# Two operands of the RWKV-7 chunk products on halves of the partitions, q ahead of the triangular inverse, and sums of squares loaded by 32 columns

## The chip, the cores and the metric

The kernel runs on one core of a Trainium2 chip. The metric is the device time of one execution in microseconds (us). The core has TensorE (PE; its weight loads are listed as PEld), VectorE (DVE), ScalarE (ACT), GpSimd (POOL) and SyncE (SP, which issues most DMAs). A tile of TensorE's array is named by rows and columns: 64*64 is one quarter, given by the half of the partitions that the operands lie on and the half that the result goes to in PSUM.

## The reference, cut to what matters

Two layers: dilated window attention, then RWKV-7 time mixing, each with attention into memory tokens, a gate and an output projection. There are 512 prompt tokens and 8 x 4 sample tokens. The change lies in the RWKV layer (12 heads of 64) and in the sums of squares of the norms.

```python
kk = k * k_k
kk = kk / jnp.maximum(jnp.sqrt(jnp.sum(kk * kk, axis=-1, keepdims=True)), 1e-12)
k = k * (1.0 + (a - 1.0) * k_a)
def step(S, inp):            # inp: r, decay, k, v, -kk, kk * a
    r_t, w_t, k_t, v_t, a_t, b_t = inp
    sa = einsum('bhvk,bhk->bhv', S, a_t)
    S = S * w_t[:, :, None, :] + sa[..., None] * b_t[:, :, None, :] + v_t[..., None] * k_t[:, :, None, :]
    return S, einsum('bhvk,bhk->bhv', S, r_t)
y = x * lax.rsqrt(jnp.mean(x * x, axis=-1, keepdims=True) + 1e-6) * g      # every norm
```

## The kernel before

All activations are held feature-major: features on partitions, the 544 tokens along the free axis. Dense products (lines 314 to 316) split weights and activations into a high and a low float32r part and add three products into one PSUM bank.

The scan of the 512 prompt tokens is done in 8 chunks `c` of 64. Two heads `h` fill one tile of 128 features; two such pairs `j` make a group `g`, so there are three groups of four heads. Per pair, `decay` and `keys` (L1289) form A, R (tile AR) and B, K (tile BK). `keys` first needs the sum of squares of each head: five matmuls named kn (L1304) load 128 tokens of the squares (the last 32) and stream the two columns of `ind2`. Norms do the same over all features in `add_squares` (L325; tiles ss, ssm, ssz).

`scores` (L1349) makes, for each chunk and head, the 64x128 products of B and of K with A and R. Masked, they stand in SA (with A) and SR (with R), index 0 from B and 1 from K; `unit` and `score` say on which half of the partitions and in which columns the block of a chunk and head lies. Then `by_token` transposes A and v into UV and B and K into BK, 128x128 at a time.

`products` (L1429) inverts the triangular 64x64 blocks of a group. A loop of 30 steps on DVE (L1477, L1479) inverts 32x32 blocks, X (L1493, L1502) joins them, and SA holds the inverse. Behind it stand, of 32 matmuls each: w, the inverse with A (L1513); q, the scores of K with v (L1528); v, the inverse with q (L1528). Each takes two PSUM banks of the tag "t", which has two buffers, and two copies. `recur` (L1640) then goes through the chunks: z takes the state `St` to the next chunk, y gives the output; DVE adds what z gave into `u` (L1703) and makes the new state (L1721).

Work is recorded by generators with ranks (class `Flow`): the one with the lowest rank that is ready goes next, and dense products fill between. The program's order is then set by a scheduler that plays the recorded program through a timeline of its own, so an edit in one place can move instructions elsewhere. `by_turns` keeps the matmuls of one token in the order written. On the chip each engine runs its own list strictly in order.

The last group's recurrence ends the RWKV layer. Dense products of the output projection stand beside it: o1 (12 records for each of 16 results; they need the gated features 0 to 3 of groups 0 and 1) and o2 (which needs group 2), then the last norm (ssz) and the stores.

Of the kernel before, what the change touches and what calls it, by code (L numbers as in the profile page):

```python
# [54 lines left out]
NT = 544  # L55
# [177 lines left out]
def _device(tc, I, O):  # L233
# [91 lines left out]
    def add_squares(acc, sq, n, first, last):  # L325

        for i in (0, 256, 128) if n > 256 else (0, 128):
            w = min(128, n - i)
            nc.tensor.matmul(acc[0:w, i // 128:i // 128 + 1], sq[:, i:i + w], ones[:, 0:1],
                             start=first and i == 0, stop=last and i == 128)  # L330
# [899 lines left out]
    def unit(c, j, h):  # L1230
        a = ((c - j) % 8 // 2 * 2 + h) * 64
        return H2[(c + j) % 2], slice(a, a + 64)


    def turned(c, j, h):
        return h ^ (c + j) % 2

    def score(c, j, h):
        a = ((c - j) % 8 // 2 * 2 + turned(c, j, h)) * 64
        return H2[(c + j) % 2], slice(a, a + 64)  # L1240

    def block(i, j, e):

        return (2 * i + j, e), ((2 * i + j + 1) % 8, 1 - e)
# [48 lines left out]
    def keys(p):  # L1293
# [8 lines left out]
        for t in range(5):  # L1302
            w = 128 if t < 4 else 32
            nc.tensor.matmul(pss[0:w, 2 * t:2 * t + 2], sq[:, t * 128:t * 128 + w], ind2, start=True, stop=True)  # L1304
# [45 lines left out]
    def scores(p):  # L1350
# [19 lines left out]
        def by_token(src0, src1, dst, dsts, name):  # L1370

            for x, (src, a) in enumerate((src0, src1)):
# [19 lines left out]

        for i in (0, 2):
            pts = [ps_t(f"sc{n}{i}{e}") for e in range(2)]
            for k in range(2):
                for x in range(2):
                    a = (2 * k + x) * 128
                    for e in (1, 0):
                        for c, h in block(i + k, j, e)[::1 - 2 * e]:
                            nc.tensor.matmul(pts[e][unit(c, j, h)[0], a:a + 128], BK[H2[h], j, x, CH[c]],  # L1400
                                             AR[H2[h], j, :, CH[c]], start=True, stop=True)
                            by_turns(f"sc{n}{i}")
# [22 lines left out]
        yield from by_token((AR.rearrange("p j x t -> p (j x t)"), 2 * j * NT), (q.xv, 0), lambda x: UV[:, x, j], st.UVs[:, j], "av")  # L1425
        flow.done(f"tokens{p}", 1.0)
        flat = BK.rearrange("p j x t -> p (j x t)")
# [3 lines left out]
    Q0, Q1 = [slice(64 * hh, 64 * hh + 32) for hh in range(2)], [slice(64 * hh + 32, 64 * hh + 64) for hh in range(2)]  # L1431

    def products(g):
# [72 lines left out]
        yield f"tokens{2 * g + 1}"  # L1506
        for e in range(2):
            pt = ps_t(f"w{g}{e}")
            for j in range(2):
                for i in range(4):  # L1510
                    for c, h in block(i, j, e):
                        a = (4 * j + i) * 64
                        nc.tensor.matmul(pt[H2[h], a:a + 64], UV[unit(c, j, h)[0], 0, j, unit(c, j, h)[1]],  # L1513
                                         SA[unit(c, j, h)[0], 0, j, score(c, j, h)[1]], start=True, stop=True)
            both[e](AR[:, :, 0, 0:512].rearrange("p j (i e t) -> p j i e t", e=2, t=64)[:, :, :, e],
                    pt.rearrange("p (j i t) -> p j i t", j=2, t=64))
            yield 1.0, 0

        u = st.u = UV[:, 0].rearrange("p j (c e v) -> p (j c) e v", c=4, e=2)
        for k in range(2):  # L1520
            for i in range(2):
                pt = ps_t(f"{'qv'[k]}{g}{i}")
                for c in range(4 * i, 4 * i + 4):
                    for j, h in PAIRS:
                        r, cs = score(c, j, h)
                        e = turned(c, j, h)
                        a = (c % 4 * 2 + e) * 64
                        nc.tensor.matmul(pt[r, a:a + 64], SA[r, 1 - k, j, cs],  # L1528
                                         u[r, c, e] if k else UV[r, 1, j, unit(c, j, h)[1]], start=True, stop=True)
                both[i](UV[:, 0, i], pt)  # L1530
                yield 1.0, 0
# [116 lines left out]
    def recur(g):  # L1648
# [19 lines left out]
        def y_of(cs, e):  # L1668
# [7 lines left out]
            for step in steps:  # L1676
                c, k, t = step
                for j, h in PAIRS:
                    if turned(c, j, h) == t:
                        r, s = score(c, j, h)  # L1680
                        lhs = SR[r, 2 - k, j, s] if k else AR[H2[h], j, 1, CH[c]]
                        rhs = (UV[r, 1, j, unit(c, j, h)[1]] if k == 1 else u[r, c, t] if k else states[c][H2[h], j ^ h])
                        y = ((c - a) * 2 + h) * 64
                        put(yps[r, y:y + 64], lhs, rhs, e and step == steps[0], not e and step == steps[-1])
# [11 lines left out]
        for c in range(8):  # L1696
            n = f"{g}_{c}"
            states.append(St)
            if c:
                for j, h in PAIRS:  # L1700
                    r, cs = score(c, j, h)
                    put(zs[r, turned(c, j, h), 0, c % 2], AR[H2[h], j, 0, cs], St[H2[h], j ^ h], True, True)
# [10 lines left out]
            for k in (1, 0):  # L1713
                for j, h in PAIRS:
                    r, cs = unit(c, j, h)
                    e = turned(c, j, h)
# [330 lines left out]
```

## Time and profile before

| | us |
|---|---|
| median of 3 runs | 797.19 |
| all runs | 796.6, 803.0, 797.19 |
| the profiled execution | 796.88 |
| its span on the core | 794.9 |
| mean granted TensorE clock | 0.976 |

A row of the profile names line, engine, operation, result and operands, then how many, and durations. In a timeline row stand the start, the time to the end of the last record, and the idle time ahead of it with what ended that. An f32 matmul of TensorE stands as two records, a transpose or a float32r matmul as one. The granted clock is the share of full clock that TensorE was given. The chain of waits is followed back from the last instruction.

### The profile page before, as it was taken

How to read it: one execution, taken by the hardware profiler on the slowest of the kernel's cores; microseconds unless marked ns; L12 is line 12 of the kernel's file. 1: busy time of each engine (PE TensorE's matmuls, PEld its weight loads, DVE VectorE, ACT ScalarE, POOL GpSimd, SP SyncE). 2: the span in 40 equal slices, each digit the busy share in tenths (PEclk: the TensorE clock that was granted, in tenths of full speed). 3: DMA queues.
4: the chain of work that ended last, by engine and by line, in shares of the span. 5: the costliest groups of instructions: out<-in, count | busy, mean ns of one | idle time of the engine just before them, and what ended most of it. 6: DMA issues, size and time to landing. Idle time of an engine off the chain costs nothing.

```text
span 794.9 us, 20301 instructions
## 1 busy us (share of the span) xinstructions
PE 740.0 (93%) x8360; PEld 631.8 (79%) x8360; DVE 444.2 (56%) x1088; ACT 338.3 (43%) x789; POOL 349.4 (44%) x389
## 2 busy tenths in 40 slices
PE   6899999999999969889999999899999999999783
PEld 5877878798976857788888889798888987888663
DVE  7743321218455574652545479837599455785456
ACT  7454421125443464447585348243644423621121
POOL 4642322332220554755444337534455345551447
PEclk9999999999999999999999999999999999999797
DMA  7465359862225571254114421210223222540103
GB/s 251 132 221 180 114 176 310 305 242 84 82 68 218 185 242 42 76 162 134 55 47 149 151 89 61 77 41 16 71 74 108 84 82 82 154 130 19 51 31 114
DMA packets 55697, 97.49 MB, mean 123 GB/s; under 512 B 6607, under 2 KB 21231, under 8 KB 55567
## 3 DMA queue, kind: packets, MB, share of 16 engines
q1 hardware_dynamic: 55604, 96.19, 37.1%
q8 instruction: 66, 1.08, 0.6%
q14 instruction: 27, 0.22, 0.1%
HBM read 82.67 MB, written 13.49 MB: 121 GB/s over the span
## 4 chain that ended last, share of the span: by engine, by line
PE 72%; DVE 12%; POOL 5%; DMA 4%; issue 3%; ACT 3%; SPq 1%; POOLq 0%; DVEq 0%; ACTq 0%
PE b_h L314 2%; PE b_h L315 2%; PE b_h L316 2%; PE o L314 2%; PE Sx L566 2%; PE o L315 2%; PE o L316 2%; PE sc L1400 2%; PE y L1663 1%; PE z L1663 1%; PE o L794 1%; PE ox L590 1%; DMA ug<-ud 1%; PE ptx L582 1%; DMA vc<-in_vc 1%
## 5 line engine op out<-in xcount | busy, mean ns | idle before, releaser
L307 POOL TENSOR_TENSOR lo_b<-raw_b,hi_b 128x512 fp32r<-128x512 f32 x58 | 77.6, 1340 | 119.8 <-ACT hi_b L306 88.2
L307 POOL TENSOR_TENSOR lo_a<-raw_a,hi_a 128x512 fp32r<-128x512 f32 x44 | 56.7, 1290 | 130.2 <-ACT hi_a L306 129.6
L306 ACT CAST hi_a<-raw_a 128x512 fp32r<-128x512 f32 x44 | 27.3, 621 | 61.7 <-DMA raw_a<-in_w_in_a 34.6
L306 ACT CAST hi_b<-raw_b 128x512 fp32r<-128x512 f32 x58 | 36.4, 628 | 38.1 <-PE b_h L316 10.0
L315 PE MATMUL b_h<-xg,lo_b 128*128 128x272 f32 x160 | 46.1, 296 | 2.0 <-POOL lo_b L307 2.0
L314 PE MATMUL b_h<-xg,hi_b 128*128 128x272 f32 x160 | 47.3, 301 | 0.0
L316 PE MATMUL b_h<-xg,hi_b 128*128 128x272 f32 x160 | 46.1, 294 | 0.0
L314 PEld LDWEIGHTS b_h<-xg,hi_b 128*128 128x128 f32 x160 | 29.8, 188 | 3.8 <-issue 2.3
L315 PEld LDWEIGHTS b_h<-xg,lo_b 128*128 128x128 f32 x160 | 29.8, 188 | 3.0 <-POOL lo_b L307 2.4
L1477 DVE TENSOR_TENSOR TX<-T,TT 128x30 f32<-128x30 f32 (+14 forms) x90 | 29.3, 326 | 3.9 <-ACT T L1451 2.2
L1479 DVE TENSOR_TENSOR T<-T,TX 128x30 f32<-128x30 f32 (+14 forms) x90 | 30.0, 333 | 1.8
L316 PEld LDWEIGHTS b_h<-xg,hi_b 128*128 128x128 f32 x160 | 29.8, 188 | 0.5
L1705 POOL TENSOR_TENSOR Sd<-St,DF 128x128 f32<-128x128 f32 x21 | 8.4, 402 | 36.5 <-DVE St L1723 19.0
L1400 PE MATMUL sc<-AR,BK 64*64 64x128 f32 x384 | 18.2, 277 | 1.9 <-DVE bv L1346 1.9
L314 PE MATMUL o<-h,hi_o1a 128*128 128x256 f32 (+1 forms) x64 | 18.7, 293 | 0.9 <-DVE z L1941 0.9
L316 PE MATMUL o<-h,hi_o1a 128*128 128x256 f32 (+1 forms) x64 | 18.4, 290 | 0.9 <-DVE h L1797 0.9
L315 PE MATMUL o<-h,lo_o1a 128*128 128x256 f32 (+1 forms) x64 | 18.4, 288 | 0.0
L786 ACT COPY PT<-pa 128x512 f32<-128x512 f32 x16 | 9.1, 586 | 21.8 <-PE pa L785 17.9
L1663 PE MATMUL y<-UV,SR 64*64 64x64 f32 x384 | 17.3, 242 | 0.0
L1400 PEld LDWEIGHTS sc<-AR,BK 64*64 64x64 f32 x384 | 12.4, 133 | 5.0 <-DVE bv L1346 2.3
L1663 PEld LDWEIGHTS y<-UV,SR 64*64 64x64 f32 x384 | 15.7, 157 | 0.3 <-issue 0.3
L1721 DVE TENSOR_TENSOR St<-z,Sd 128x128 f32<-128x128 f32 x21 | 6.0, 286 | 16.2 <-PE z L1663 11.6
(1066 smaller groups left out, 2796.2 us busy)
## 6 DMA issues: line engine op xcount, KB each, us to landing
raw_b<-in_w_in_b SPq DMA_DIRECT2D x58, 256.0 KB, 2.7
raw_a<-in_w_in_a SPq DMA_DIRECT2D x44, 256.0 KB, 2.8
kc<-in_kc SPq DMA_DIRECT2D x18, 512.0 KB, 6.4
vc<-in_vc SPq DMA_DIRECT2D x18, 512.0 KB, 7.6
out_win<-t SPq DMA_DIRECT2D x12, 272.0 KB, 3.0
x<-in_x SPq DMA_DIRECT2D x8, 272.0 KB, 5.4
xr<-in_x SPq DMA_DIRECT2D x16, 136.0 KB, 4.2
x1d<-z SPq DMA_DIRECT2D x2, 1088.0 KB, 5.2
```

The lines of the kernel that those rows point to most:

```text
L306: nc.scalar.copy(hi, raw)
L307: lo_eng.tensor_tensor(lo, raw, hi.bitcast(F32), ALU.subtract)
L314: nc.tensor.matmul(ps[:, :n], hi, xh, start=first, stop=False)
L315: nc.tensor.matmul(ps[:, :n], lo, xh, start=False, stop=False)
L316: nc.tensor.matmul(ps[:, :n], hi, xl, start=False, stop=last)
L566: nc.tensor.matmul(S[hh][64 * e:64 * e + 64, 0:256], qm[r, f, a:a + 64], kT[l][r, f, :], start=True, stop=True)
L786: nc.scalar.copy(PT[hh], pa.rearrange("p (j q) -> p j q", j=4))
L1400: nc.tensor.matmul(pts[e][unit(c, j, h)[0], a:a + 128], BK[H2[h], j, x, CH[c]], AR[H2[h], j, :, CH[c]], start=True, stop=True)
L1477: nc.vector.tensor_tensor(pd, TP[:, 0:s, s:s + 1].to_broadcast([128, s, w]), TT[:, s:s + 1, s + 1:32].to_broadcast([128, s, w]), ALU.mult)
L1479: nc.vector.tensor_tensor(TP[:, 0:s, s + 1:32], TP[:, 0:s, s + 1:32], pd, ALU.add)
L1663: nc.tensor.matmul(out, lhs, rhs, start=start, stop=stop)
L1705: nc.gpsimd.tensor_tensor(Sd, St, DF[:, :, c:c + 1].to_broadcast([128, 2, 64]), ALU.mult)
```

## The change

Five edits:

1. `add_squares` and kn load 32 columns at a time and write to partitions 0, 32, 64 and 96 in turn: kn has 17 matmuls in place of 5, the squares of the last norm 27 and 24 in place of 9 and 6.
2. The scores with A of head 1 go to the other half of the partitions than those with R. For that the 64x128 product with B is cut in two of 64x64; ten matmuls take the place of eight.
3. A and v are transposed by half tiles (64 rows, 128 tokens) in `two_by_two`, so that A of head 1 lands on the other half. 17 or 19 matmuls take the place of 8 or 10.
4. q moves out of `products` into `early_q`, begun when A and v of the group's second pair have been transposed. Its result `u` goes into the place of the scores in SA, which so lives until the recurrence ends; before, `u` was in UV.
5. In `products` v comes ahead of w, both in the order of `PAIRS` with all four quarters in turn; v uses the two banks "zs" and w two of "t".

The recurrence has the same matmuls with other indices.

```diff
     def add_squares(acc, sq, n, first, last):
         for i in (0, 256, 128) if n > 256 else (0, 128):
-            w = min(128, n - i)
-            nc.tensor.matmul(acc[0:w, i // 128:i // 128 + 1], sq[:, i:i + w], ones[:, 0:1],
-                             start=first and i == 0, stop=last and i == 128)
+            for a in range(0, min(128, n - i), 32):
+                w = min(32, n - i - a)
+                nc.tensor.matmul(acc[a:a + w, i // 128:i // 128 + 1], sq[:, i + a:i + a + w], ones[:, 0:1],
+                                 start=first and i == 0, stop=last and i == 128)
...
+    def low(c, j, h=0):
+        return (c + j + h) % 2
+    def slot(c, e):
+        a = (c // 2 * 2 + e) * 64
+        return slice(a, a + 64)
+    def tokens(c, j, h, odd):
+        a = ((c - odd) % 8 // 2 * 2 + h) * 64
+        return slice(a, a + 64)
     PAIRS = ((0, 0), (1, 1), (1, 0), (0, 1))
...
-            nc.tensor.matmul(pss[0:w, 2 * t:2 * t + 2], sq[:, t * 128:t * 128 + w], ind2, start=True, stop=True)
+            for a in range(0, 128 if t < 4 else 32, 32):
+                nc.tensor.matmul(pss[a:a + 32, 2 * t:2 * t + 2], sq[:, t * 128 + a:t * 128 + a + 32], ind2, start=True, stop=True)
...
+        def two_by_two():
...
+            for x, (src, a) in enumerate(((src0, a0), (src1, a1))):
+                for i in range(4):
+                    for h, r in enumerate(H2):
+                        odd = low(0, j, 0 if x else h)
+                        o_, b = pts[h][:, (4 * x + i) * 64:(4 * x + i) * 64 + 64], a + 128 * i + 64 * odd
...
+                        nc.tensor.transpose(o_, src[r, b:b + o_.shape[0]], ident[r, r])
...
             for k in range(2):
-                for x in range(2):
-                    a = (2 * k + x) * 128
-                    for e in (1, 0):
-                        for c, h in block(i + k, j, e)[::1 - 2 * e]:
-                            nc.tensor.matmul(pts[e][unit(c, j, h)[0], a:a + 128], BK[H2[h], j, x, CH[c]],
-                                             AR[H2[h], j, :, CH[c]], start=True, stop=True)
+                cs, a = (2 * (i + k), 2 * (i + k) + 1), 256 * k
+                for c in cs:
+                    piece(0, c, 0, None, low(c, j), a)
+                    piece(1, c, 0, 0, low(c, j, 1), a)
+                for c in cs:
+                    piece(1, c, 0, 1, low(c, j), a)
+                for c in cs:
+                    for h in range(2):
+                        piece(h, c, 1, None, low(c, j), a + 128)
...
         flow.done(f"tokens{p}", 1.0)
+        if j:
+            flow.spawn(RANK[3], early_q(g))
...
+    def early_q(g):
+        st.u = SA[:, 1].rearrange("p j (c e v) -> p (j c) e v", c=4, e=2)
+        pts = [ps_t(f"q{g}{b}") for b in range(2)]
+        for c in range(8):
+            for j, h in PAIRS:
+                b = low(c, j)
+                nc.tensor.matmul(pts[b][H2[low(c, j, h)], 64 * c:64 * c + 64], SA[H2[b], 1, j, slot(c, h)],
+                                 UV[H2[b], 1, j, tokens(c, j, h, j)], start=True, stop=True)
+        for b in range(2):
+            both[b](st.u[:, :, b], pts[b].rearrange("p (c v) -> p c v", v=64))
...
-        yield f"tokens{2 * g + 1}"
+        yield f"q{g}"
+        pt = ps_zs(f"v{g}").rearrange("p (e c v) -> p e c v", e=2, v=64)
+        for c in range(8):
+            for j, h in PAIRS:
+                e = low(c, j, h)
+                nc.tensor.matmul(pt[H2[low(c, j)], e, c], SA[H2[e], 0, j, slot(c, h)], u[H2[e], c, low(c, j)],
+                                 start=True, stop=True)
         for e in range(2):
-            pt = ps_t(f"w{g}{e}")
...
+            both[e](u[:, :, e], pt[:, e])
+        pts = [ps_t(f"w{g}{e}") for e in range(2)]
...
```

Three places of TensorE's list show what moves. The first is the first product X of the last group's inverse (X from TX and SA) among the dense o1 products (o from h and hi_o1a or lo_o1a). Before:

```order
L315 MATMUL o_10011<-h_9766,lo_o1a_10008 128x256
L316 MATMUL o_10011<-h_9766,hi_o1a_10007 128x256
L1493 MATMUL X_8923<-TX_8474,SA_7479 32x32 x32
L314 MATMUL o_10025<-h_9766,hi_o1a_10007 128x288
L315 MATMUL o_10025<-h_9766,lo_o1a_10008 128x288
```

And now:

```order
L315 MATMUL o_10100<-h_9985,lo_o1a_10083 128x288
L316 MATMUL o_10100<-h_9985,hi_o1a_10082 128x288
L1546 MATMUL X_9069<-TX_8624,SA_7616 32x32 x32
L314 MATMUL o_10124<-h_9985,hi_o1a_10120 128x256
L315 MATMUL o_10124<-h_9985,lo_o1a_10121 128x256
```

Before, X stood behind the thirteenth of the 16 results of o1, with 132 dense records left behind it in the program; now it stands behind the sixth, with 216 left. Recurrence 1's last z had 407 left and now has 450.

The second place is the end of the same inverse (X from SA and TX) and the products behind it. Before:

```order
L1502 MATMUL X_8973<-SA_7479,TX_8474 32x32 x32
L316 MATMUL o_10063<-h_9766,hi_o1a_10045 128x288
L1513 MATMUL w_9020<-SA_7479,UV_7481 64x64
L1513 MATMUL w_9038<-SA_7479,UV_7481 64x64
L1513 MATMUL w_9020<-SA_7479,UV_7481 64x64 x15
L1513 MATMUL w_9038<-SA_7479,UV_7481 64x64 x15
L1541 MATMUL q2s<-UVs_7483,SAs_7484 32x64 x4
L1528 MATMUL q_9056<-UV_7481,SA_7479 64x64 x16
L1528 MATMUL q_9074<-UV_7481,SA_7479 64x64 x16
L1539 MATMUL w2s<-SAs_7484,UVs_7483 64x32
L1528 MATMUL v_9101<-UV_7481,SA_7479 64x64 x16
L1528 MATMUL v_9119<-UV_7481,SA_7479 64x64 x16
```

And now, behind 24 dense records that follow X:

```order
L316 MATMUL o_10196<-h_9985,hi_o1a_10192 128x256
L1565 MATMUL v_9189<-SA_7616 64x64 x2
L1575 MATMUL w_9224<-SA_7616,UV_7618 64x64 x2
L1565 MATMUL v_9189<-SA_7616 64x64 x30
L1575 MATMUL w_9225<-SA_7616,UV_7618 64x64 x4
L1575 MATMUL w_9224<-SA_7616,UV_7618 64x64 x4
```

q is gone from here, v stands ahead of nearly all of w, and the recurrence's first z follows w; five more results of o1 (60 records) come between its steps.

The third place is the sum of squares kn of the fifth pair among dense products. Before:

```order
L316 MATMUL b5h_7659<-xg_3427,hi_b_7654 128x272
L1304 MATMUL kn_7239<-ind_4288,BK_7003 128x2 x4
L1304 MATMUL kn_7239<-ind_4288,BK_7003 32x2
L314 MATMUL b17h_8122<-xg_3427,hi_b_8112 128x272
L315 MATMUL b17h_8122<-xg_3427,lo_b_8113 128x272
```

And now:

```order
L315 MATMUL b_h_8526<-xg_3475,lo_b_0_8516 128x272
L316 MATMUL b_h_8526<-xg_3475,hi_b_0_8515 128x272
L314 MATMUL b_h_8526<-xg_3475,hi_b_1_8521 128x272
L1302 MATMUL kn_7364<-ind_4336,BK_7023 32x2 x17
L1627 MATMUL gn0s<-ident,yc0s 64x64 x2
```

The 17 small matmuls stand together. SP's list has the load of x1 into SA's buffer behind the store of the last state, where it stood ahead of it, and only stores stand behind it; DVE's list has 31 other instructions inside the last inverse's loop, where it had 36.

More of the change, by code (lines that the diff above doesn't have):

```diff
@@ L1391, in by_token @@
             yield 0.3, 0
+        def two_by_two():
+            (src0, a0), (src1, a1) = (AR.rearrange("p j x t -> p (j x t)"), 2 * j * NT), (q.xv, 0)
+            pts = [ps_t(f"av{n}{h}") for h in range(2)]
+            for x, (src, a) in enumerate(((src0, a0), (src1, a1))):
[3 more added lines that the diff above has]
+                        o_, b = pts[h][:, (4 * x + i) * 64:(4 * x + i) * 64 + 64], a + 128 * i + 64 * odd
+                        if odd and i == 3:
+                            if a:
+                                nc.tensor.transpose(o_, src[r, a - 64:a + 64], ident[r, r])
+                            else:
+                                nc.tensor.matmul(o_[64:128], src[r, 0:64], ident[r, r], start=True, stop=True)
+                            by_turns(f"av{n}")
+                            o_ = o_[0:64]
+                        nc.tensor.transpose(o_, src[r, b:b + o_.shape[0]], ident[r, r])
+                        by_turns(f"av{n}")
+                if not x:
+                    yield 0.5, 0
+            for h in range(2):
+                nc.scalar.copy(UV[:, :, j].rearrange("p x (i e t) -> p x i e t", e=2, t=64)[:, :, :, h],
+                               pts[h].rearrange("p (x i t) -> p x i t", x=2, t=64))
+            yield 0.5, 0
+            yield from by_token((src0, a0), (src1, a1), None, st.UVs[:, j], "av")
@@ L1393, in scores, with piece @@
+        def piece(h, c, x, k, half, a):
+            o_ = a + 64 * (k or 0)
+            rhs = AR[H2[h], j, :, CH[c]] if k is None else AR[H2[h], j, k, CH[c]]
+            nc.tensor.matmul(pts[h][H2[half], o_:o_ + (128 if k is None else 64)], BK[H2[h], j, x, CH[c]], rhs,
+                             start=True, stop=True)
+            by_turns(f"sc{n}")
         for i in (0, 2):
-            pts = [ps_t(f"sc{n}{i}{e}") for e in range(2)]
+            pts = [ps_t(f"sc{n}{i}{h}") for h in range(2)]
@@ L1519, in products @@
[L1519 to L1531, printed above, removed]
+        yield f"q{g}"
@@ new lines, in products @@
+        for c in range(8):
+            for j, h in PAIRS:
+                e, a = low(c, j, h), (4 * j + c // 2) * 64
+                nc.tensor.matmul(pts[e][H2[h], a:a + 64], UV[H2[e], 0, j, tokens(c, j, h, low(0, j, h))],
+                                 SA[H2[e], 0, j, slot(c, h)], start=True, stop=True)
+                by_turns(f"w{g}")
+        for e in range(2):
+            both[1 - e](AR[:, :, 0, 0:512].rearrange("p j (i e t) -> p j i e t", e=2, t=64)[:, :, :, e],
+                        pts[e].rearrange("p (j i t) -> p j i t", j=2, t=64))
```

52 lines of the change are left out of this document (21 added, 31 removed).

## The prediction

> **What bounds the kernel now.** I read the page first: busy shares, slices, and the shares of the chain that ended last.
>
> ```profile
> span 794.9 us, 20301 instructions
> ...
> PE 740.0 (93%) x8360; PEld 631.8 (79%) x8360; DVE 444.2 (56%) x1088; ACT 338.3 (43%) x789; POOL 349.4 (44%) x389
> ...
> PE   6899999999999969889999999899999999999783
> ...
> PEclk9999999999999999999999999999999999999797
> ...
> PE 72%; DVE 12%; POOL 5%; DMA 4%; issue 3%; ACT 3%; SPq 1%; POOLq 0%; DVEq 0%; ACTq 0%
> ```
>
> TensorE holds 72% of the chain, so an instruction saved there counts almost anywhere before the last slices. Then the table by stretches, cut at the marks of the last RWKV group (its inverse starts at 676.4, its first product stands at 718.0, its recurrence runs from 734.1 to 758.9):
>
> ```profile
> core 0: us, PE busy (x) PEld busy (x) DVE busy (x) ACT busy (x) POOL busy (x), PEclk, DMA share, GB/s
> 380.00:500.00 120.00, 119.67 (x1080) 103.56 (x1079) 73.86 (x204) 70.47 (x181) 56.25 (x58) 1.00 0.29 95
> 500.00:676.40 176.40, 170.55 (x2709) 150.02 (x2708) 114.25 (x282) 65.99 (x148) 83.01 (x93) 0.97 0.23 70
> 676.40:718.00 41.60, 37.98 (x333) 36.06 (x332) 34.95 (x98) 17.66 (x39) 22.87 (x19) 1.00 0.49 140
> 718.00:734.10 16.10, 15.24 (x390) 14.00 (x390) 7.68 (x14) 3.46 (x7) 2.31 (x3) 1.00 0.01 3
> 734.10:758.90 24.80, 19.67 (x417) 15.47 (x418) 11.99 (x34) 3.24 (x9) 10.79 (x15) 0.79 0.16 55
> 758.90:794.90 36.00, 21.18 (x184) 18.21 (x183) 22.30 (x56) 8.27 (x21) 21.48 (x28) 0.81 0.21 72
> ```
>
> Until 718 TensorE is full. In the last recurrence it is idle for 5.1 us of 24.8, at a granted clock of 0.79: there the latency of the recurrence is the limit, and no dense product is left to fill it. What leads there, from the chain of waits and DVE's timeline:
>
> ```profile
> 715.83 2.04 DVE TX L1487
> 717.86 0.14 issue
> 718.00 1.20 PE X L1493 x63
> ...
> 724.33 1.15 PE X L1502 x64
> 725.50 0.69 DVE SA L1504
> 726.21 0.58 ACT SA L1504
> 726.80 0.14 issue
> 726.93 1.87 PE w L1513 x58
> ...
> 729.14 2.01 PE q L1528 x64
> ...
> 731.38 2.01 PE v L1528 x64
> ...
> 734.08 0.29 DVE L1723 COPY St<-z 128x128 f32<-128x128 f32 x1
> ...
> 758.93 0.28 DVE L1721 TENSOR_TENSOR St<-z,Sd 128x128 f32<-128x128 f32 x1
> ```
>
> From SA's last copy (726.8) to the first state (734.1) go 7.3 us, of them 5.9 in w, q and v.
>
> **Prices.** TensorE's timeline gives the pace of starts; an f32 matmul stands as two records, and the duration of a record overlaps its neighbours, so starts count.
>
> ```profile
> 520.97 0.29 PE L316 MATMUL b4h<-xg,hi_b 128*128 128x272 f32 x1
> 521.09 0.29 PE L314 MATMUL b4h<-xg,hi_b 128*128 128x272 f32 x1
> 521.31 1.91 PE L1513 MATMUL w<-SA,UV 64*64 64x64 f32 x64
> ...
> 533.43 0.46 PE L1663 MATMUL z<-UV,BK 64*64 64x64 f32 x16
> ...
> 193.04 0.63 PE L845 MATMUL sC<-kn,qbd 128*32 128x32 f32 x48
> ```
>
> Less some 0.22 us for the last record to end, w goes at (1.91-0.22)/63 = 27 ns a start; it alternates between two quarters. z stands on all four: (0.46-0.22)/15 = 16 ns. sC loads 32 columns at a time: (0.63-0.22)/47 = 8.7 ns. A dense record takes 0.12 to 0.13 us; a change to another shape of tile costs about 0.22-0.12 = 0.1 us.
>
> **The change, part by part.**
>
> *w, q, v on four quarters.* 64 records at 16 ns and 0.22 make 1.23 us against 2.01: 0.78 less in each of nine stages. For groups 0 and 1, whose neighbours fill TensorE, six stages: -4.7 us (0 if they go on at 27 ns). In group 2, q is done ahead of the inverse, where TensorE is full: +1.2.
>
> *Squares of the heads (kn) and of the rows.*
>
> ```profile
> 433.52 0.94 PE kn L1304 x10
> ...
> 534.14 1.14 PE kn L1304 x10
> ...
> 768.55 1.07 PE ssz L329 x8
> ...
> 780.33 2.24 PE ssz L329 x18
> ...
> L329 PE MATMUL ssm<-ones,mraw x16: 168/250/251, 31.7 to 33.3; 128*128 128x1 f32 x16
> ```
>
> kn: 5 loads of 128 columns become 17 of 32, 34 records at 8.7 ns: 0.3 us and two changes of shape, 0.5 against 1.04. Six times: -3.2. In the tail 18 records become 54 (0.7 against 2.24) and the eight shown of twelve become 48 (0.65 against 1.07): -2.0, both on the chain. ssm falls by about 0.9, of which the start-up leaves perhaps 0.4; the squares of x stand there too and I give them nothing.
>
> *Scores and tokens*, now that A and q lie on halves:
>
> ```profile
> 602.06 1.02 PE sc L1400 x28
> ...
> 425.25 0.60 PE L1376 MATMUL av<-ident,xv 128*128 128x128 f32 x4
> ```
>
> Scores: ten matmuls replace eight, since A and R of one head part: 96 records more, by 1.02/28 = 36 ns at most 3.5 us, but four quarters are already in use and each streams as many columns as before, so 0 is the other end, and I take +0.5. Tokens: a transpose starts every (0.60-0.28)/3 = 0.11 us; 8 or 10 of them become 17 or 19 on half the rows. Side by side they cost the same, one behind another 1 us more a pair: 0 to +6, nearest the first by z's row; with their changes of shape +1.5.
>
> So until the last inverse: -4.7+1.2-3.2-0.4+0.5+1.5 = -5.1 us.
>
> *The last group.* The rows of TensorE's order show the largest move: behind the last inverse's first product stand 216 dense records where there were 132. These 84, at 0.126 us, are 10.6 us of work that moves from ahead of the inverse's end into the recurrence that had none. The first product comes that much earlier if the inverse is ready:
>
> ```profile
> L1477 DVE TENSOR_TENSOR TX<-T,TT 128x30 f32<-128x30 f32 (+14 forms) x90 | 29.3, 326 | 3.9 <-ACT T L1451 2.2
> L1479 DVE TENSOR_TENSOR T<-T,TX 128x30 f32<-128x30 f32 (+14 forms) x90 | 30.0, 333 | 1.8
> ...
> 674.78 0.29 DVE L1721 TENSOR_TENSOR St<-z,Sd 128x128 f32<-128x128 f32 x1 [1.67 <-PE z L1663]
> ...
> 676.35 0.19 DVE L1477 TENSOR_TENSOR TX<-T,TT 128x30 f32<-128x30 f32 x1 [1.14 <-ACT T L1451]
> ```
>
> Its loop needs (29.3+30.0)/3 = 19.8 us of DVE and took 39.5 (676.35 to 715.83), with 36 other DVE instructions between; now there are 31. The loop begins at the end of recurrence 1, which moves ahead by 43 of the 84 records; for the other 41 (5.2 us) the loop itself must be shorter. DVE had 6.7 us idle in that stretch. A wait of 0 to 5 us: +2.5.
>
> From SA's copy to the first state: v and w, 2.2 us, then z and its copy, 0.7, in place of 7.3; but 24 dense records stand ahead of v and outlast the copies by 1.6. Together -2.8. The recurrence with 60 dense records in it (7.5 us, for which 5.1 were idle): 0 to +5, taken +2.5. Copies of v, q and w out of PSUM are as many as before. SA2 is now held to the end of the recurrence, and a load of x1 into its buffer moves behind it on SP; only stores stand behind that load, and it is wanted some 20 us later: 0.
>
> Sum: -5.1-10.6+2.5-2.8+2.5-2.0 = -15.5 us. The profiled execution took 796.9 (its span and 2.0), 0.3 under the median of 797.2, so 781.
>
> [...] z's 16 records start 16 ns apart, sC's 8.7. [...]
>
> **Rivals.**
>
> *The inverse is not ready* and X waits for DVE's loop: all that was moved is lost, 8.1 us more than I took, 789. For it: DVE was 34.95 of 41.6 us busy. Against: five instructions fewer, and the loop's own share is half. 13%.
>
> *The quarters do not run together*: starts stay at w's 27 ns. Then +4.7 (w, q, v), +3.3 (kn: 34 at 27 ns are 0.9 us), +1.9 (ssz), +0.7 (q moved ahead), +1.4 (v and w): 793, no change. For it: w itself, already on two quarters, reaches no more. Against: z and sC. 8%.
>
> *Slower: changes of shape.* The 32-column squares and half-row transposes are another shape than the dense records; a visit costs about 0.2 us for both changes. Where the order scatters them among dense ones, each piece pays. It decides from (15.5+8)/0.2 = 118 visits more than now. For it: the squares of x are cut in three visits. Against: kn's 17 stand in one row. 805 and more; 4%.
>
> **How the numbers follow.** My forecast, 72%: 781, by its own bounds (-7 for wait and stretch; +4.5, +3 and +5 for tokens, scores, waits, not all at once) 774 to 789. The rivals at 789 and 793 have 21%, the slower one 4%, 3% is for an order that goes wrong elsewhere. The range, 772 to 792, holds the forecast and the first rival with 2 to 3 us beyond their ends, since several terms are taken inside wide bounds; it leaves out the rest, with what passes those bounds about 2 in 10. About 1% (8 us) is what a measurement here can tell from no change: under 789.2 lie the forecast and a part of the first rival, 75%; 19% within 1%; 6% slower.
>
> **What would show it.** w, q and v at 16 ns a start, kn at 0.5 us; X's first product at about 704 and waiting under 3 us; the recurrence with dense records inside and a clock near 1; ssz under 0.8 us at the end. It is wrong if TensorE waits at X for more than 8 us, if av takes over 1.5 us a pair, or if v goes at 27 ns.

## The result, and the profile after

| | median us | runs | ratio to before, 95% interval | profiled execution, span, clock |
|---|---|---|---|---|
| before | 796.89 | 20 | 1 | 796.88, 794.9, 0.976 |
| after | 804.56 | 20 | 1.0088 [1.0062, 1.0113] | 802.49, 800.7, 0.966 |

The forecast was 781 in a range of 772 to 792. The kernel did not become faster; it became slower by 0.9%, inside the 1% that the forecast called no change. None of the three rivals, at 789, 793 and 805, happened either, as the rows below show; that the time lies beside the third is chance, since the changes of shape which that rival priced are not where the time went.

The page of the changed kernel, its lines on span, busy shares and slices:

```profile
span 800.7 us, 21209 instructions
...
PE 731.5 (91%) x8828; PEld 622.6 (78%) x8828; DVE 449.5 (56%) x1088; ACT 337.3 (42%) x789; POOL 352.7 (44%) x389
...
PE   6899999999999979889999998899999888989773
...
PEclk9999999999999989999999998999899998999996
```

TensorE is busy for 8.5 us less than before (731.5 against 740.0) and the span is 5.8 us longer. So work was saved, and idle time of TensorE, 14.3 us more, took its place. In its second half the row PE has six slices with an 8 where it had two, and PEclk shows an 8 in four of its 40 slices where it showed none. A table by stretches of the changed kernel, TensorE's column only, cut at the first product of the last inverse (720.29), the first and the last state of the last recurrence (735.55 and 764.76):

```profile
core 0: us, PE busy (x), PEclk, DMA share, GB/s
...
485.00:720.29 235.29, 212.80 (x3270) 0.95 0.24 76
720.29:735.55 15.26, 13.96 (x341) 1.00 0.28 88
735.55:764.76 29.21, 23.72 (x478) 1.00 0.03 12
764.76:800.70 35.94, 19.98 (x261) 0.78 0.30 101
```

And the same of the kernel before, with marks at the same events:

```profile
...
485.00:718.00 233.00, 223.53 (x3154) 0.98 0.28 83
718.00:734.08 16.08, 15.22 (x390) 1.00 0.01 3
734.08:758.93 24.85, 19.72 (x417) 0.79 0.16 54
758.93:794.90 35.97, 21.15 (x184) 0.81 0.21 72
```

The first row of each table carries the answer. From 485 us to the first product of the last inverse TensorE is busy 10.7 us less, as the forecast wanted, but idle for 22.5 us where it was 9.5, and at a mean clock of 0.95 for 0.98. These are the stretches at half clock inside it, first of the changed kernel, then of the kernel before:

```profile
491.04:497.87 6.83, 4.66 (x40) 0.50 0.25 79
569.55:576.38 6.83, 6.66 (x39) 0.50 0.19 70
624.16:627.58 3.42, 3.42 (x26) 0.50 0.29 81
661.71:668.53 6.82, 4.31 (x27) 0.50 0.14 41
```

```profile
504.88:508.29 3.41, 3.41 (x18) 0.50 0.46 159
535.60:539.01 3.41, 3.41 (x72) 0.50 0.10 35
579.97:583.38 3.41, 3.41 (x18) 0.50 0.05 10
```

If half of TensorE's busy time there is lost, that is 9.5 us (half of 19.0) against 5.1 (half of 10.2); this is an estimate. Without that loss the work in the stretch is 203.3 us against 218.4: some 15 us of work have left it, near the forecast's 15.7 (5.1 saved and 10.6 moved). 13.0 us of waits and 4.4 us of clock came in. The first product stands 2.3 us later instead of 13.2 earlier.

What TensorE waits for: a table of waits of the changed kernel (result and line, engine waited for; us in total, times, longest).

```profile
PE gn L1624 <- DVE yc L1615: 5.2, 4, 2.7
...
PE b_h L314 <- DVE u L1212: 3.2, 2, 2.0
...
PE z L1713 <- DVE SA L1753: 2.2, 1, 2.2
PE lo L1275 <- DVE rv L1306: 2.2, 1, 2.2
...
PE kn L1302 <- ACT BK L1297: 1.8, 1, 1.8
```

All rows of that table together hold 58.5 us, against 44.6 before; 33.0 against 20.4 are waits for DVE. From 485 us to the first product no single wait is over 2.7 us. DVE has hardly more work (449.5 us against 444.2), but TensorE reaches its results before DVE has come to them. One such place, on TensorE's timeline of the changed kernel:

```profile
490.76 0.52 PE L1302 MATMUL kn<-ind,BK 128*32 128x2 f32 x34 [1.81 <-ACT BK L1297]
491.21 0.59 PE L1275 MATMUL lo<-lora,wh 128*128 128x272 f32 x1
...
494.20 0.56 PE L1275 MATMUL lo<-lora,wh 128*128 128x272 f32 x1 [2.17 <-DVE rv L1306]
```

kn is short now, 0.52 us. Its result lies in a PSUM buffer of the tag "t", which has two. The products named lo take the other, and the next lo waits until DVE's `rv` has read kn. DVE's list at that time:

```profile
491.62 1.26 DVE L1333 SCALAR_TENSOR_TENSOR xr<-xr,pv,kf 128x544 f32<-128x544 f32 x1
...
493.85 0.15 DVE L1305 TENSOR_SCALAR rv<-kn 128x8 f32<-128x8 f32 x1
```

kn ended at 491.28; its reader, 0.15 us long, began at 493.85, behind L1333 and five pieces of the inverse's loop that stand ahead of it in DVE's list. In the traces of both kernels DVE's 1064 instructions other than memsets, and ACT's 734, begin in the order of the program. TensorE stood for 1.81 us ahead of kn and for 2.17 us ahead of lo. From 491.04 to 497.87, so already before the second wait, it ran at half clock (the first of the rows above): the starts of the dense records are 0.23 us apart instead of 0.126. That costs some 2.3 us more, half of the 4.66 us.

It is not the short kn that makes this place costly. In a_nosq below, the changed kernel with kn by 128 columns again, TensorE stands at the same two instructions for 4.67 us instead of 3.98:

```profile
495.32 2.02 PE L1301 MATMUL kn<-ind,BK 128*128 128x2 f32 x10 [4.35 <-ACT BK L1296]
...
498.40 0.57 PE L1274 MATMUL lo<-lora,wh 128*128 128x272 f32 x1 [0.32 <-DVE rv L1305]
```

And in b_sq, whose kn is as short (0.48 us at 480.68), lo follows it at 481.09 without a wait.

The move of the last inverse failed through waits of the same kind, in recurrence 1. Two waits on TensorE's timeline:

```profile
660.79 0.34 PE L1713 MATMUL z<-UV,BK 64*64 64x64 f32 x8 [2.21 <-DVE SA L1753]
...
664.22 1.08 PE L1624 MATMUL gn<-ident,yc 128*128 128x128 f32 x4 [2.65 <-DVE yc L1615]
```

And DVE's timeline there:

```profile
659.18 0.43 DVE L1214 TENSOR_TENSOR u<-u,om 128x272 f32<-128x272 f32 x1
...
660.45 0.28 DVE L1753 TENSOR_TENSOR SA<-z,SA 128x128 f32<-128x128 f32 x1
...
661.11 1.52 DVE L1214 TENSOR_TENSOR u<-u,om 128x272 f32<-128x272 f32 x1
662.55 1.52 DVE L1615 TENSOR_TENSOR yc<-yc,gst 128x512 f32<-128x512 f32 x1
...
678.46 0.29 DVE L1770 TENSOR_TENSOR St<-z,Sd 128x128 f32<-128x128 f32 x1 [2.42 <-PE z L1713]
...
680.52 0.19 DVE L1530 TENSOR_TENSOR TX<-T,TT 128x30 f32<-128x30 f32 x1
```

The recurrence's addition to `u` (L1753) is behind gates and norms of other work in DVE's list; the state after it (and gn) stands behind two instructions of 1.52 us. The last state of recurrence 1 stands at 678.46, 3.7 us later than before, and the inverse's loop begins 4.2 us later. The loop ends with this row:

```profile
718.10 2.05 DVE L1540 STREAM_TRANSPOSE TX<-T 128x1024 f32<-128x1024 f32 x1
```

From its first instruction (680.52) to there the loop took 37.6 us, where it took 39.5 before (676.35 to 715.83). The first product X began 0.14 us behind its end, at 720.29, as it did before, at 718.00. So DVE's loop sets the place of X in both kernels, and the 84 dense records moved behind X could win no more ahead of it than the loop did: 1.9 us.

### The profile page after: what moved, and what is told of

The parts are those of the page before. It is cut to its first block, busy times and chain, and to the rows that moved or that the text cites. A ratio compares the mean times of both kernels' runs of the same rounds, so it can differ in the third digit from the quotient of the medians.

```text
span 800.7 us, 21209 instructions
## 1 busy us (share of the span) xinstructions
PE 731.5 (91%) x8828; PEld 622.6 (78%) x8828; DVE 449.5 (56%) x1088; ACT 337.3 (42%) x789; POOL 352.7 (44%) x389
## 3 DMA queue, kind: packets, MB, share of 16 engines
q1 hardware_dynamic: 55604, 96.19, 36.1%
## 4 chain that ended last, share of the span: by engine, by line
PE 70%; DVE 12%; POOL 6%; ACT 4%; DMA 3%; issue 3%; SPq 1%; POOLq 0%; ACTq 0%; DVEq 0%
PE b_h L314 2%; PE b_h L315 2%; PE b_h L316 2%; PE sc L1420 2%; PE o L314 2%; DMA raw_o1a<-in_w_out_b 1%; PE o L795 1%; PE Sx L567 1%; PE o L316 1%; PE y L1713 1%; PE o L315 1%; PE ssz L1006 1%; PE z L1713 1%; PE ox L591 1%; PE pa L786 1%
## 5 line engine op out<-in xcount | busy, mean ns | idle before, releaser
L306 ACT CAST hi_b<-raw_b 128x512 fp32r<-128x512 f32 x58 | 36.3, 626 | 36.9 <-PE b_h L316 21.5
L314 PEld LDWEIGHTS b_h<-xg,hi_b 128*128 128x128 f32 x160 | 30.8, 194 | 5.3 <-DVE u L1212 3.6
L316 PEld LDWEIGHTS b_h<-xg,hi_b 128*128 128x128 f32 x160 | 30.7, 194 | 0.3
L1455 POOL TENSOR_TENSOR BK<-BK,DT 128x512 f32<-128x512 f32 x12 | 13.2, 1111 | 19.5 <-PE sc L1420 19.5
L1420 PE MATMUL sc<-AR,BK 64*64 64x64 f32 (+1 forms) x480 | 18.6, 255 | 0.5 <-DVE SR L1441 0.3
L314 PE MATMUL o<-h,hi_o1a 128*128 128x288 f32 (+1 forms) x64 | 18.9, 297 | 0.2 <-DVE z L1990 0.2
L315 PE MATMUL o<-h,lo_o1a 128*128 128x256 f32 (+1 forms) x64 | 18.2, 290 | 0.0
L316 PE MATMUL o<-h,hi_o1a 128*128 128x256 f32 (+1 forms) x64 | 18.1, 289 | 0.0
L307 POOL TENSOR_TENSOR lo_mem<-raw_mem,hi_mem 128x512 fp32r<-128x512 f32 x8 | 12.8, 1598 | 8.5 <-ACT hi_mem L306 7.4
L1614 POOL TENSOR_TENSOR gst<-gst,mhalf 128x8 f32<-128x8 f32 (+1 forms) x7 | 10.3, 1473 | 14.1 <-DVE gst L1613 13.9
```

Of the source, the lines that this page charges most:

```text
L306: nc.scalar.copy(hi, raw)
L307: lo_eng.tensor_tensor(lo, raw, hi.bitcast(F32), ALU.subtract)
L314: nc.tensor.matmul(ps[:, :n], hi, xh, start=first, stop=False)
L315: nc.tensor.matmul(ps[:, :n], lo, xh, start=False, stop=False)
L316: nc.tensor.matmul(ps[:, :n], hi, xl, start=False, stop=last)
L1420: nc.tensor.matmul(pts[h][H2[half], o_:o_ + (128 if k is None else 64)], BK[H2[h], j, x, CH[c]], rhs, start=True, stop=True)
```

## The experiments

All ratios are to the kernel before, run on the same chip, with 95% intervals. "First product" is the first X of the last inverse; idle time and clock of TensorE are those from 485 us to there, in the profiled execution. Of a kernel whose edit changes the work, the scheduler orders all instructions anew, so each run differs from its neighbour by the edit and by an order. Only batches in several planner settings can tell the two apart.

**First: how much is order alone?** Two numbers of the planner, RHO (how much dense work is due for each unit of other work) and DEBT (the debt from which a dense product goes first), are changed in both kernels; the work stays the same.

```diff
# b_rho34, a_rho34
-RHO, DEBT = 0.35, 0.54
+RHO, DEBT = 0.34, 0.54
# b_debt5, a_debt5
-RHO, DEBT = 0.35, 0.54
+RHO, DEBT = 0.35, 0.50
```

> The kernel before, with one number of the planner moved (RHO 0.35 to 0.34): the same instructions, another order from the middle of the RWKV layer on (some 13% of DVE's list stands elsewhere). Order theory (the change shortened TensorE's list, and the waits of a newly laid order took it back): a new order without any change of work costs this kernel too, 801 to 812 us, with new waits of TensorE for DVE between 560 and 740. Rival, form theory (the new forms of the products bring the waits, the order does not matter much): 797 within 4 us.

> The changed kernel with the same number moved (RHO 0.35 to 0.34). Order theory: the time moves by more than 4 us one way or the other (790 to 815), and the waits of recurrence 1 (gn for yc, z for SA, together 7 us) are gone or stand elsewhere. Form theory: 804.5 within 4 us, with the same waits at the same instructions.

> The kernel before with another number of the planner moved (DEBT 0.54 to 0.50). Order theory: 801 to 812 us. Form theory: 797 within 4 us.

> The changed kernel with DEBT 0.54 to 0.50, which lays the order anew from the second group's start on. Order theory: off 804.5 by more than 4 us either way, the waits between 485 and 680 at other instructions. Form theory: 804.5 within 4 us, with the same waits.

| | ratio | first product | idle | clock |
|---|---|---|---|---|
| before / b_rho34 / b_debt5 | 1 / 1.0017 [0.9984, 1.005] / 1.0038 [1.0, 1.0076] | 718.0 / 716.3 / 723.7 | 9.5 / 9.9 / 10.0 | 0.98 / 0.96 / 0.95 |
| after / a_rho34 / a_debt5 | 1.0088 / 1.0154 [1.01, 1.0208] / 0.9917 [0.9888, 0.9946] | 720.3 / 727.5 / 710.6 | 22.5 / 21.2 / 15.8 | 0.95 / 0.93 / 0.98 |

The kernel before hardly answers to its order (by ratio the order theory's 801 to 812 us were missed there: the kernel before itself had a median of 799.5 us beside these runs). The changed one answers by 2.4%, and form theory fails for it: with DEBT at 0.50 the same work is 0.8% faster than before. So "slower by 0.9%" is a result of this one order of the instructions. The stretch in a_debt5, to be read against the row from 485 us in each table by stretches above:

```profile
485.00:710.64 225.64, 209.84 (x3275) 0.98 0.26 79
```

Here too TensorE is idle for 15.8 us, more than in any order of the kernel before. So more idle time comes with the change in all three orders; how much of it depends on the order.

**Second: which part?** The squares alone on the kernel before (kn, ss, ssm and ssz by 32 columns; edit 1 of the change), and three kernels that undo one part of the changed one.

```diff
# b_sq, on the kernel before: edit 1 of the change
# a_ss128: the squares of the start-up (ss, ssm) by 128 again
+                add_squares(acc, sq[0][:, k], 256, k == 0, k == 3, 128)
+                add_squares(acc, sums[h][:, k], HF, k == 0, k == 1, 128)
# a_lateq: q behind the inverse again
-            flow.spawn(RANK[3], early_q(g))
...
-        yield f"q{g}"
+        yield f"tokens{2 * g + 1}"
+        yield from early_q(g)
# a_db_ss128: a_ss128 with DEBT 0.50
```

> The kernel before with only the squares (kn, ss, ssm and ssz) loaded by 32 columns. Theory 1 (the 32-column squares save what was forecast, but in the start-up the new order lets TensorE wait past two microseconds twice, and each such wait is followed by some 3.4 us at half clock): kn takes 0.3 us in place of 1.04; in the first 60 us TensorE waits 2.3 us at a19h and 2.2 at mkv as in the changed kernel (1.1 and 1.5 before), with dense records starting 0.23 us apart behind them, and 3 to 4 us of the start-up are lost; the whole within 4 us of before. Rival (the start-up waits come from something else in the change): both waits as before, and 791 to 794 us.

> The changed kernel with the squares of the start-up alone (ss, ssm) loaded by 128 columns again, kn and the last norm by 32. Theory 1: the two waits of the start-up fall back to 1.1 and 1.5 us, no half clock before 280 us, and what stands at 165 us in the start-up's order comes 3 to 4 us earlier than in the changed kernel, beside the waits; the order behind is laid anew, so the whole lies anywhere from 790 to 808. Rival: the waits stay.

> The changed kernel with q back behind the inverse, ahead of v. Theory of the order: nothing hangs on q itself; SA's last copy to the first state takes about 1.3 us longer than in the changed kernel, and the waits between 485 and 680 fall at other instructions, 793 to 812 us. Rival (q ahead of the inverse holds two PSUM banks while DVE is in the loop and so makes TensorE wait for DVE): the waits for DVE between 485 and 680 fall from about 19 us to below 10, and the time to under 796.

> The changed kernel with DEBT 0.50 (0.992 of before) and the squares of the start-up at 128 columns. If the start-up's 4 us are to be had beside a good order: 0.985 to 0.989 of before, 788 us. If the new order behind it is a bad one: 0.995 to 1.01.

| | median us | ratio | first product | idle | clock |
|---|---|---|---|---|---|
| b_sq | 789.75 | 0.9884 [0.983, 0.9938] | 707.4 | 9.3 | 1.00 |
| a_ss128 | 799.7 | 1.0037 [1.0006, 1.0067] | 715.4 | 18.2 | 0.97 |
| a_lateq | 801.36 | 1.0019 [0.9979, 1.006] | 725.1 | 19.3 | 0.94 |
| a_db_ss128 | 801.1 | 1.0029 [0.9991, 1.0067] | 712.3 | 19.7 | 0.95 |

The squares alone make the kernel 1.2% faster, and both expectations of b_sq were missed: the two waits of the start-up are there (2.0 and 2.3 us), but the clock behind them stayed at 1.00. The stretch of b_sq:

```profile
485.00:707.38 222.38, 213.05 (x3190) 1.00 0.29 86
```

TensorE is busy there as long as in the changed kernel (213.05 against 212.80), but at a clock of 1.00 instead of 0.95 and idle for 9.3 us instead of 22.5, so its first product stands 12.9 us earlier. Taking q back or the start-up's squares back leaves 18 to 20 us idle: neither is where the idle time comes from. By the ends of the intervals, a_lateq is 0.0 to 1.3% below the changed kernel and a_ss128 -0.1 to 1.1%; one order each, which by the first batch proves little. That a_ss128 and a_debt5 each lie below the changed kernel and together (a_db_ss128) do not, says the same.

**Third: the rest without the squares, and the squares in other orders.** a_nosq is the changed kernel with all squares by 128, so halves, four quarters and early q alone; b_sq in the two other planner settings; b_kn with only kn by 32.

```diff
# a_nosq, on the changed kernel (add_squares likewise)
-            for a in range(0, 128 if t < 4 else 32, 32):
-                nc.tensor.matmul(pss[a:a + 32, 2 * t:2 * t + 2], sq[:, t * 128 + a:t * 128 + a + 32], ind2, start=True, stop=True)
+            w = 128 if t < 4 else 32
+            nc.tensor.matmul(pss[0:w, 2 * t:2 * t + 2], sq[:, t * 128:t * 128 + w], ind2, start=True, stop=True)
# b_kn, on the kernel before: the same lines with - and + exchanged
```

> The changed kernel with all squares loaded by 128 columns as before: the halves and the early q alone. The squares alone gave 0.988 of before. If the rest of the change costs by itself (its own work or the waits that it brings): 1.01 to 1.03 of before, with waits of TensorE for DVE and ACT between 485 and 680 of 12 us and more. If the rest is worth the 5 us that was forecast and only the order of the changed kernel was a bad one: 0.98 to 1.00.

> The kernel before with the 32-column squares, and RHO 0.34: is the gain of the squares one of work or of a lucky order? Work (about 9 us less for TensorE, whatever the order): 0.985 to 0.995 of before. Luck: 1.00 and more.

> The same with DEBT 0.50. Work: 0.985 to 0.995 of before. Luck: 1.00 and more.

> The kernel before with kn alone by 32 columns (the start-up and the last norm as before). kn was forecast at 0.5 us for 1.04, six times, 3.2 us: 0.996 of before if the order gives it through; the start-up as in the kernel before; the last norm at 1.07 and 2.24 us as before. If the rest of the 0.988 of the squares comes from the last norm and the start-up, 0.993 to 0.999 here.

| | median us | ratio | first product | idle | clock |
|---|---|---|---|---|---|
| a_nosq | 815.91 | 1.0206 [1.0138, 1.0274] | 728.9 | 19.3 | 0.94 |
| b_sq_rho34 | 793.65 | 0.993 [0.9896, 0.9964] | 713.4 | 10.5 | 0.98 |
| b_sq_debt5 | 795.12 | 0.9953 [0.9922, 0.9985] | 717.2 | 7.9 | 0.99 |
| b_kn | 790.89 | 0.9884 [0.9837, 0.9931] | 709.5 | 9.5 | 1.00 |

The squares gain 0.5 to 1.2% in all three orders, and in the one order in which kn was tried alone it has all of it, against the 0.1 to 0.7% that were expected. Edits 2 to 5 without them cost 2.1%, in one order. Set on top of the squares in the same three settings, they cost 2.1% (1.0088/0.9884; from 1.2 to 2.9 by the ends of the intervals), 2.3% (1.4 to 3.2) and, with DEBT 0.50, -0.4% (-1.0 to +0.2).

**Fourth: what in edits 2 to 5?** `two_by_two` fills two banks with A and v at once, and both are full only at its end; `by_token` filled one and copied it while the next was filled. b_sq_avmix takes that one property into b_sq, with whole transposes and no halves, in three settings. a_q8 lets the early q of the changed kernel go with the rank of late work.

```diff
# b_sq_avmix, on b_sq (in by_token, for A and v)
+                pts = [ps_t(f"{name}{n}{x}") for x in range(2)]
+                for i in range(4):
+                    for pt, (src, a) in zip(pts, (src0, src1)):
...
+                            nc.tensor.transpose(pt[:, 128 * i:128 * i + 128], src[:, b:b + 128], ident)
+                        by_turns(f"av{n}")
...
+                for x, pt in enumerate(pts):
+                    nc.scalar.copy(dst(x), pt)
# b_sq_avmix_db: with DEBT 0.50; b_sq_avmix_rho: with RHO 0.34
# a_q8, on the changed kernel
-            flow.spawn(RANK[3], early_q(g))
+            flow.spawn(8, early_q(g))
```

> The kernel before with the 32-column squares (0.988 of before), and one thing more: the transposes of A and v of a pair are taken in turn, so that both of their PSUM banks are full only at the end; before, the bank of A is copied out while v is transposed. The products, their shapes and their number stay. Bank theory (in the changed kernel A and v by half tiles fill both banks of the tag t together; what uses these banks next, and the chain of the next pair behind it, comes later in TensorE's list, dense products go ahead and are missing afterwards): TensorE waits 48 us or more in all where the squares alone have 45, and 0.992 to 1.00 of before. Rival (it is the scores on halves or the early q): 44 to 46 us of waits and 0.985 to 0.991.

> The same in the order of DEBT 0.50 (the squares alone there: 0.995 of before, 44 us of waits). Bank theory: 47 us or more, 0.999 to 1.007. Rival: 43 to 45 us, 0.992 to 0.998.

> The same in the order of RHO 0.34 (the squares alone there: 0.993 of before, 46 us of waits). Bank theory: 49 us or more, 0.997 to 1.005. Rival: 45 to 47 us, 0.990 to 0.996.

> The changed kernel with q still ahead of the inverse, but of the lowest rank beside the dense products, so that it no longer stands between the two banks of B and K. If q's place there holds up the next pair: waits fall by 3 us and more from 58, and the time to 1.000 of before or less. If not: waits of 54 and more, 1.004 and more.

| | median us | ratio | first product | idle | clock |
|---|---|---|---|---|---|
| b_sq_avmix | 798.32 | 1.0012 [0.9983, 1.0041] | 724.6 | 14.1 | 0.96 |
| b_sq_avmix_db | 796.93 | 0.9985 [0.9956, 1.0014] | 718.9 | 10.4 | 0.97 |
| b_sq_avmix_rho | 797.8 | 1.0007 [0.9976, 1.0037] | 720.7 | 19.1 | 0.93 |
| a_q8 | 811.72 | 1.0182 [1.0145, 1.022] | 737.0 | 26.8 | 0.93 |

In each setting the kernel with both banks filled together is behind its neighbour with the squares alone: by 1.3% (0.5 to 2.1), 0.3% (-0.3 to 0.9) and 0.8% (0.1 to 1.4). The work is the same to the instruction. In all three the kernel is back at the time before, so the squares' gain is gone; and the mean of the three, 0.8%, is more than half of what edits 2 to 5 cost on the mean (1.3%). In the trace, though, the added waits stand at many places and not at the transposes. This is the stretch of b_sq_avmix_rho:

```profile
485.00:720.71 235.71, 216.61 (x3177) 0.93 0.26 80
```

In its table of waits z stands for DVE's St for 4.6 us in four pieces, and b17h for DVE's xr for 4.0 in one. So the cost of the property is shown, in two settings of three beyond the intervals; that the banks themselves are what is waited for is not. It may be the order that comes of it. In a_q8 the later place in the queue for q makes the kernel 0.9% slower still (0.3 to 1.6), in the one order tried.

**Fifth: the remaining parts.** b_sq_ss128 leaves the start-up's squares by 128, with kn and ssz by 32; b_sq_sc10 takes edit 2's ten score products (the 64x128 product with B of head 1 cut in two) into b_sq, without halves.

```diff
# b_sq_ss128, on b_sq: the two lines of a_ss128
# b_sq_sc10, on b_sq
-                            nc.tensor.matmul(pts[e][unit(c, j, h)[0], a:a + 128], BK[H2[h], j, x, CH[c]],
-                                             AR[H2[h], j, :, CH[c]], start=True, stop=True)
+                            for k2 in ((0, 1) if h and not x else (None,)):
+                                rhs = AR[H2[h], j, :, CH[c]] if k2 is None else AR[H2[h], j, k2, CH[c]]
+                                o_ = a + 64 * (k2 or 0)
+                                nc.tensor.matmul(pts[e][unit(c, j, h)[0], o_:o_ + (128 if k2 is None else 64)],
+                                                 BK[H2[h], j, x, CH[c]], rhs, start=True, stop=True)
```

> The kernel before with kn and the squares of the last norm (ssz) by 32 columns, those of the start-up by 128. The list of every engine is that of b_kn but for the ssz pieces, so nothing else moves. The forecast took 2.0 us of the end for ssz: 0.986 of before where b_kn had 0.988, and the last stretch from the last state to the end 2 us shorter than b_kn's. Rival (the end waits for DVE, ACT and POOL behind the squares, not for TensorE): ssz shrinks by 2 us, the waits behind it grow by as much, and 0.988 as b_kn.

> The kernel before with the 32-column squares (0.988) and the scores of the changed kernel as to number: of the eight products of a chunk pair, those of B with head 1 are cut in two of 64x64, ten for eight, 96 records more, in place. The forecast took 0.5 us of TensorE (0 to 3.5): 0.986 to 0.995 of before, waits of 44 to 47 us. Rival (the cut scores bring the rest of what the halves cost): 0.997 and more, waits of 48 and more.

| | median us | ratio | first product | idle | clock |
|---|---|---|---|---|---|
| b_sq_ss128 | 791.68 | 0.9893 [0.9841, 0.9944] | 713.9 | 9.7 | 0.99 |
| b_sq_sc10 | 795.14 | 0.9975 [0.994, 1.001] | 713.7 | 9.7 | 0.99 |

b_sq_ss128 cannot be told from b_sq or b_kn: ssz and the start-up's squares bring nothing that can be measured. b_sq_sc10 is 0.9% (0.0 to 1.8) behind b_sq. By its numbers the rival came true (0.997 and more, waits of 48.1 us in all), but the ratio lies near the spread that order alone gives to the squares (0.988 to 0.995), and the stretch has no more idle time. One order: inconclusive.

The best kernels of the study are b_sq, b_kn and b_sq_ss128, at 0.988 to 0.989 of the time before; they beat both kernels. All three keep edit 1 or a part of it and nothing else.

## Why the prediction was wrong

*The prices held.* Rows of the changed kernel:

```profile
473.12 1.16 PE L1477 MATMUL q<-UV,SA 64*64 64x64 f32 x62
...
720.29 1.20 PE L1546 MATMUL X<-TX,SA 32*32 32x32 f32 x64 [0.30 <-DVE TX L1540]
...
731.64 1.15 PE L1565 MATMUL v<-SA 64*64 64x64 f32 x60
732.62 1.10 PE L1575 MATMUL w<-SA,UV 64*64 64x64 f32 x60
```

q starts every (1.16-0.22)/61 = 15.4 ns, v and w 15.8 and 14.9; 16 was forecast. By this the rival of quarters that do not run together falls. kn's 34 records took 0.52 us, where 0.5 was forecast: a start every (0.52-0.22)/33 = 9.1 ns. X waited 0.3 us for the inverse, not 8, so the rival of an inverse that is not ready did not happen as it was described; but X began right behind DVE's loop, so the loop was what held it, and it began late because recurrence 1 ended late. The rival of shape changes did not happen as a mechanism, since TensorE's work at full clock fell by about what was forecast. The half transposes do not explain the loss either: those of group 0's two pairs took 1.4 and 1.8 us, the whole ones 1.3 and 1.8.

*The failing step* was the first one: "Until 718 TensorE is full", and from it "an instruction saved there counts almost anywhere". The row behind it (170.55 us busy of 176.40) was right for the kernel before. The forecast took it over for the changed kernel, whose order nobody had measured. Of its -15.5 us it gave -5.6 to the squares and -9.9 to edits 2 to 5, and in these its only price for a wait was the +2.5 at the last inverse; the +1.5 for tokens and +0.5 for scores are TensorE's own time. Measured, the work left as forecast, but +13.0 of waits and +4.4 of clock came into the stretch. They come with the halves: all nine kernels without halves and without the mixed banks have 8 to 10.5 us idle in that stretch, all eight with halves 16 to 27.

That a shortened TensorE must run into such waits is not what the runs show: b_sq and b_kn are shortened as well, have no more idle time than the kernel before, and are faster. For the squares "counts almost anywhere" held. What in edits 2 to 5 brings the waits is shown only for the banks filled together, and there without the mechanism; that TensorE, in the order laid out for them, comes to the strict lists of DVE and ACT too early is a reading of the places above.

*Point by point, in us, forecast against measured:*

| step | forecast | measured |
|---|---|---|
| until the last inverse's first product | -13.2 | +2.3 |
| from there to the first state | -2.8 | -0.8 (16.08 to 15.26) |
| the last recurrence | +2.5, bounds 0 to 5 | +4.4 (24.85 to 29.21) |
| the end | -2.0 | 0.0 (35.97 to 35.94) |
| sum | -15.5 | +5.8 of the span |

The first line is the forecast's -5.1, -10.6 and +2.5 together. Of the 15.5 us by which it misses, 14.2 arose ahead of recurrence 1's last state: by the forecast that moves ahead by 10.5 (5.1, and 43 records at 0.126 us), and it stands 3.7 later. The loop behind it was to give 2.7 and gave 1.4. The recurrence came out as its mechanism said, dense records inside and the clock at 1.00, with its size near the upper bound. The first state gained less: v began 11.1 us behind X instead of the forecast's 10.4, and from there to the state it took 4.2 us instead of 2.9, since z had to wait for ACT's copy of v (to 734.19) and then paused for 0.5 us.

The end gained nothing because the chain stepped to another engine. Before, the 18 records of ssz for 2.24 us stood on it. Now, in the chain of waits:

```profile
783.06 0.82 POOL sq L1907
...
786.51 1.71 POOL z L1875 x3
...
789.99 0.94 PE ssz L357 x3
```

Four squares on POOL (783.06 to 786.51) stand at that place, beside which the matmuls of ssz are hidden. The forecast had put both ssz terms "on the chain" and did not ask what was next in line. b_sq_ss128, which differs from b_kn in ssz alone and is not faster, agrees: its end, from the last state on, is 0.8 us shorter than b_kn's (36.1 against 36.9), not 2.0.

*The squares* were mis-sized the other way: -3.2 for kn, -0.4 and -2.0 were forecast; alone they bring 0.5 to 1.2%, 4 to 9 us, and kn alone 9 us in its order. The price of kn held even so. Reckoned as above, b_kn's stretch holds 3.4 us less work than that of the kernel before. The other 5.1 us by which its first product is earlier are the clock: none of the stretch ran at half clock, where the kernel before lost 5.1 us. This is one execution of each; whether such a gain comes from the order or from chance is not shown.

*What stays open.* The cost of edits 2 to 5 (2.1, 2.3 and -0.4%) could not be split into a sum of parts. Filling both banks at once is shown to cost 0.3 to 1.3% in a kernel without halves; the cut scores, early q and the larger sensitivity to order may hold the rest, and each part was tried in one order only. Whether a scheduler that knew the waits would win the forecast's 15 us was not tried.

## What to carry to other kernels

That the busiest engine is full is a property of one order of the instructions. Before pricing a change on it, ask where the engine takes results from another's strict list and what the change does to these places; here 15 us of work left as forecast, and 13 us of waits and 4 us of clock took their place. Where a scheduler lays out the program anew for each edit, run the kernel before and after in two or three orders of the same work before a per cent is believed; here order alone moved the changed kernel by 2.4%. And change one part at a time: the cheapest edit of this change was worth 0.5 to 1.2% by itself, and the rest took it away.

## What the runs showed of the hardware

A wait of TensorE of 2.04 us was followed by half clock in the changed kernel, one of 2.05 us at the same instruction in b_sq was not; they differ in when they fall. In the traces of the kernel before and of the changed one the granted clock changes only at whole multiples of 3.41 us from its first change (15 and 19 changes). In the start-up the same wait stands in the changed kernel and in b_sq; first the changed kernel's, on TensorE's timeline, and two stretches of that grid (columns as in the tables by stretches):

```profile
22.72 0.39 PE L314 MATMUL a19h<-xg,hi_a 128*128 128x272 f32 x1 [2.04 <-DVE o L492]
```

```profile
20.01:23.42 3.41, 1.37 (x11) 1.00 0.00 0
23.42:26.83 3.41, 3.41 (x17) 0.50 0.21 70
```

And the same of b_sq, with three stretches of its grid:

```profile
22.96 0.39 PE L314 MATMUL a19h<-xg,hi_a 128*128 128x272 f32 x1 [2.05 <-DVE o L492]
```

```profile
17.96:21.38 3.42, 2.95 (x29) 1.00 0.03 9
21.38:24.79 3.41, 1.83 (x14) 1.00 0.00 0
24.79:28.20 3.41, 2.98 (x37) 1.00 0.51 134
```

In the changed kernel the 2.04 us fall into one stretch, TensorE is busy for 1.37 us of it, and the next runs at half clock. In b_sq the 2.05 us are divided between two, which are busy for 2.95 and 1.83 us, and the clock stays at 1.00. In the traces of the kernel before and of the changed one, from 13.4 us on, where the records of the clock begin, the least busy stretch that full clock follows was busy for 1.73 us (757.28 to 760.69 in the changed kernel). Half clock also followed a stretch that was busy throughout: in the kernel before the one from 532.19 was busy for 3.41 us of 3.41, and the one from 535.60 ran at 0.50. So the busy time of a stretch does not decide it alone. The list of the changed kernel is the same in all its 20 executions, and their mean clock lies between 0.956 and 0.971, their time between 800.2 and 808.4 us.

The same addition on DVE (`u`, L1214, 128x272) took 0.43 us at 659.18 and 1.52 us at 661.11, where POOL ran a split of 1.25 us from 661.08, and the recurrence waited behind the second: its state (L1770) stands at 664.35. What made the second longer is not shown. In the kernel before, the same addition (L1213) took 0.44 us at 650.78, where POOL ran a split of 1.52 us from 650.84.
